# A hybrid decoder layer on one core: 2x2 block products for the convolution's inputs, one row of weight buffers, attention outputs kept in DRAM

## The chip, the core and the metric

The kernel runs on one core of a Trainium2 chip. The core has a matrix engine (TensorE, PE in the profile; its weight loads are shown as PEld), a vector engine (VectorE, DVE), a scalar engine (ScalarE, ACT), a general engine (GpSimd, POOL) and a queue engine (SyncE, SP). Each runs its own instruction queue in order, and they meet at semaphores. PE reads SBUF and accumulates into PSUM banks of 128 x 512 floats; DVE and ACT read and write both; DMA queues, fed here by SP and POOL, move data between DRAM and SBUF. The metric is the device time of one execution in microseconds (us), lower being better.

## What is computed

One decoder layer over 512 tokens with 16 learned meta tokens in front of them (528 positions), model width 2048, all in float32:

```python
n = _rmsnorm(h, g_mix[l])
p = n @ w_in[l]
q, k, v, gb, gc, u = jnp.split(p, ...)
o_attn = _stick_breaking_attention(q, k, v).reshape(b, L, ATTN_WIDTH)
o_conv = gb * _causal_dwconv(gc * u, conv_w[l])
o = jnp.concatenate([_rmsnorm(o_attn, g_attn_out[l]),
                     _rmsnorm(o_conv, g_conv_out[l])], axis=-1)
h = h + o @ w_out[l]
n2 = _rmsnorm(h, g_ffn[l])
h = h + (jax.nn.silu(n2 @ w_gate[l]) * (n2 @ w_up[l])) @ w_down[l]
return h[:, N_META:]
```

Each of q, k, v, b (`gb`), c (`gc`) and u is 1024 wide: 8 heads or channel blocks of 128. The convolution has three taps, so position t needs c*u at t-2, t-1 and t. The FFN is 5632 wide.

## The kernel before

**Layout and products.** Everything is held transposed: channels on the 128 partitions, tokens along the free axis. A float32 operand is split into a high part that PE takes in one pass (`float32r`) and the rest (a cast on ACT, a subtraction on DVE: `split`, L194). A product of weights W and activations a is the sum of W_hi a_hi, W_hi a_lo and W_lo a_hi: three matmuls for each 128 x 128 tile of weights and each stretch of up to 512 columns. The weights arrive as float32 by SP's queue and are split in the kernel as well.

**Stages**, in the order in which PE runs them:

- *Input.* x times `g_mix` is split into 16 pairs of tiles, `n_parts` (`nh`, `nl`, L226), one for each 128 of the 2048 model channels. The RMS factor `r` of each token and its square `r2` are applied to the products when they are taken out of PSUM.
- *Attention*, eight heads (`head`, L355): k, q and v by `product` (L190), which walks the 16 tiles of `n_parts`; then `attend` (L382), whose parts are threaded between the next head's matmuls by `after` and `tick`. Its output o (L491 to L496) is scaled and split into `oa_all`, which stays in SBUF until the output projection.
- *Convolution*, eight channel blocks (L532 to L560): c and u by `cu_product` (516 columns as 256 and 260: 16 tiles x 3 x 2 = 96 matmuls each), multiplied; three taps; b (512 columns, 48 matmuls); the product with b on POOL; the split into `oc_all`; the sum of squares `acc_c`. The parts of the last head's attention run under c, u and b of block 0. `scale_a` (L519) makes the attention group's RMS factor.
- *Output projection* (L562 and L839 on): for each of 16 output tiles one product over the attention half and one over the convolution half (48 matmuls of 512 columns in all), then the residual, and the activations of the FFN as *block products* want them.
- *FFN*: gate and up, then down, by `pair_product` (L756). It takes a 2 x 2 block matrix of weights times a 2 x 2 block matrix of activations (two halves of the contraction, two halves of the 512 tokens) in seven products of blocks instead of eight. For that, sums and differences of weight blocks (`add_quads`, `add_last`: four additions for each pair) are made on DVE, and sums and differences of activation blocks are kept beside the blocks themselves (`acts`, seven of them).

**Weights.** Until the first output tile, weights go through `stream`: tiles `raw` of eight 128 x 128 blocks (two of them), split in pieces of four blocks, four pieces ahead (`prepare`, L137; `next_w`, L152). From then on they go through two long tiles, `sw_in` (six places of eight blocks) and `sw_split` (three places for pairs of high and low parts), eight blocks at a time and two pieces ahead (`split_quad`, L651; `prepare_pair`, L677).

**Order.** The instructions are laid into each engine's queue by a scheduler that goes by the program's order, with preparation of weights at high priority. Space in SBUF is a stack of pools from either end: a pool opened where another was released waits, tile by tile, for what lay there (`reuse_waits="tile"`).

Of the kernel before, what the change touches and what calls it, by code (L numbers as in the profile page):

```python
# [15 lines left out]
P = 128  # L16
# [17 lines left out]
def hybrid_layer(ctx: ExitStack, tc: tile.TileContext, xT, w_in, w_out, w_gu, w_down, vecs, out):  # L34
# [67 lines left out]
    stream = []  # L102

    OUT_TILES = [k + 8 * half for k in range(8) for half in (1, 0)]

    WIDE_AT, PARTS_AT = 16, 48

    def plan_w(src, n, at=PARTS_AT):  # L110
        stream.append((src, n, at))

    FIRST = ((0, 2), (2, 4), (4, 8), (8, 12), (12, 16))
    for a, b in FIRST:
        for c in (8, 0):
            plan_w(w_in[c, a // 8][:, (a % 8) * P : (a % 8 + b - a) * P], b - a, PARTS_AT if c else WIDE_AT)
    for j in range(HEADS):
        for c in (8 + j, j, 16 + j)[0 if j else 2 :]:
            for b in range(2):
                plan_w(w_in[c, b], 8, WIDE_AT if c == j else PARTS_AT)  # L120
    for j in range(HEADS):
        for c in (32 + j, 40 + j, 24 + j):
            for b in range(2):
                plan_w(w_in[c, b], 8, WIDE_AT if c == 24 + j else PARTS_AT)
    for b in range(2):
        plan_w(w_out[OUT_TILES[0], b], 8)
    raws, ready, taken = [], [], [0]
    SUB, AHEAD = 4, 4
    subs = [(i, a, min(a + SUB, n)) for i, (_, n, _) in enumerate(stream) for a in range(0, n, SUB)]

    def load_raw(pool=wpool, cols=8 * P, **kw):
        i = len(raws)
        src, n, _ = stream[i]
        raws.append(pool.tile([P, cols], F32, name=f"raw{i}", **kw))
        tc.keep_in_program_order(nc.sync.dma_start(raws[i][:, : n * P], src))

    def prepare():  # L137
        i, a, b = subs[len(ready)]
        with tc.high_priority():
            if i == len(raws):  # L140
                load_raw(tag="raw", bufs=2)
            raw, c = raws[i][:, a * P : b * P], (b - a) * P
            at = stream[i][2]
            hi, lo = (
                wpool.tile([P, SUB * P + 64], F32R, tag=t, bufs=AHEAD + 1, name=f"{t}{i}_{a}")[:, at : at + c]
                for t in ("whi", "wlo")
            )
            sc.copy(hi, raw)  # L148
            ve.tensor_tensor(lo, raw, hi.bitcast(F32), ALU.subtract)  # L149
        ready.append((hi, lo, b - a))  # L150

    def next_w():  # L152
        i = taken[0]
        taken[0] += 1
        while len(ready) < min(len(subs), i + 1 + AHEAD):
            prepare()
        hi, lo, n = ready[i]
        return [(hi[:, k * P : (k + 1) * P], lo[:, k * P : (k + 1) * P]) for k in range(n)]
# [14 lines left out]
    def product_steps(parts, acts, n):  # L173

        k, last = 0, n - 1
        while k <= last:

            ws = next_w()
# [38 lines left out]

    accp = open_pool("accp")
    oapool = open_pool("oapool")
    rpool = open_pool("rpool", side="right")  # L220
    xpool = open_pool("xpool", KT, side="right")
    raw_first = open_pool("raw_first", side="right")
# [3 lines left out]
    n_parts = [[npool.tile([P, L + 48], F32R, name=f"{t}{k}") for t in ("nh", "nl")] for k in range(KT)]  # L226
    npool.tile([P, 8], F32, name="pad_n")
# [60 lines left out]

    for a, b in FIRST:
        for i in range(2):  # L290
            load_raw(raw_first, (b - a) * P)
            if a == i == 0:
                load_x(0)
        for k in range(max(a, 1), b):
            load_x(k)
    for a, b in FIRST:
        for k in range(a, b):
            split_x(k)
        for step in steps:
            next(step)  # L300
# [7 lines left out]
    raw_first.release()  # L308
# [11 lines left out]
    def o_slots(pool, name):  # L320

        t = pool.tile([P, 2 * HEADS * SEQ], F32R, name=name)
        return t.rearrange("p (h a t) -> p h a t", h=HEADS, a=2)

    oa_all = o_slots(oapool, "oa")
    oa = []

# [54 lines left out]
    def attend(h, kn, kh, kl, qn, qh, ql, vt):  # L382
# [98 lines left out]
        def mix(ws):  # L481
# [14 lines left out]
            oa.append((oh, ol))  # L496
# [22 lines left out]
    def scale_a():  # L519
        sh, sl = (tmp.tile([P, SEQ], F32R, tag=t, bufs=2, name=f"{t}_a") for t in ("e", "e2"))  # L520
        token_scale(acc_a, acc_a, 1024, "a", (sh, sl, t512(SEQ, "v", 2)[:, :SEQ], None, None))


    C0, CN = 12, L - 12
    oc = []

    def cu_product(name):
        ps = pp.tile([P, 2, 512], F32, tag="pp", name=name).rearrange("p a b -> p (a b)")
        product([(ps[:, T2:512], C0, C0 + T2), (ps[:, 512 : T2 + CN], C0 + T2, L)], n_hl)
        return ps[:, T2 : T2 + CN]  # L530

    for j in range(HEADS):  # L532
        pc = cu_product(f"pc{j}")
        cu = t512(CN, "e", 2)[:, :CN]
# [34 lines left out]
    wpool.release()  # L569
    npool.release()  # L570

# [560 lines left out]
```

## Time and profile before

| what | value |
|---|---|
| median of 3 runs | 2058.72 us (2058.11 to 2059.23) |
| span of the profiled execution | 2056.9 us |
| attention, first matmul of k to first of c of block 0 | 5.6 to 339.5 us |
| c and u of block 0 to the last b | 339.5 to 616.0 us |
| output projection | 616.0 to 790.6 us |
| FFN, gate and up | 790.6 to 1632.8 us |
| FFN, down | 1632.8 to 2053.1 us |

The profile is of one execution. Its span runs from the first to the last instruction; about 1.8 us of a run's time lie outside it. For each engine it gives the time in which it was busy. Matmuls are pipelined and their ends are modelled, so PE's busy time says that PE had work, not how fast it went; the pace is seen from the number of matmuls in a stretch. A row of instructions reads: line, engine, operation, output<-inputs, shapes, count | busy us, mean ns of one | idle time of the engine just before them, and what ended it. A row of DMA issues reads: destination<-source, queue, count, KB each, median us from issue to landing.

### The profile page before, as it was taken

What the parts mean: (1) busy time and instruction counts of PE and PEld (TensorE: products, weight loads), DVE (VectorE), ACT (ScalarE), POOL (GpSimd) and SP (SyncE); (2) the same over time, 40 slices, a digit from 0 to 9 for tenths busy, and PEclk for the clock granted to TensorE, in tenths of its full rate; (3) what the DMA queues carried; (4) which work ended last, traced back from release to release, by engine and by line L of the source; (5) the groups of instructions that cost most, each with busy time, mean ns of one, the idle gap of its engine ahead of it and who ended that gap; (6) DMA issues with size and microseconds to landing.
All of it is one profiled execution on the core that took longest, in us unless ns stands there. A gap on an engine that the chain in (4) does not pass through costs nothing.

```text
span 2056.9 us, 39370 instructions
## 1 busy us (share of the span) xinstructions
PE 2046.7 (100%) x16086; PEld 1976.0 (96%) x16086; DVE 1623.2 (79%) x2146; ACT 1016.0 (49%) x1529; POOL 351.5 (17%) x484
## 2 busy tenths in 40 slices
PE   9999999999999999999999999999999999999999
PEld 9899999999998888999999999999999999999999
DVE  7877767533336668999898898888888988888888
ACT  7666666322224344555555555555555544444443
POOL 0111111010103442111011011011011243131211
PEclk9999999999999999999999999999999999999999
DMA  5122222222235556556555465465455899798864
GB/s 198 63 83 72 80 75 76 94 93 93 95 103 168 169 173 201 160 148 190 155 162 166 145 176 158 148 175 154 144 175 164 257 338 348 186 300 208 218 149 94
DMA packets 141669, 326.74 MB, mean 159 GB/s; under 512 B 12256, under 2 KB 60128, under 8 KB 141488
## 3 DMA queue, kind: packets, MB, share of 16 engines
q1 hardware_dynamic: 67456, 212.50, 31.8%
q0 software_dynamic: 74032, 111.73, 21.1%
q8 instruction: 126, 2.06, 0.4%
q14 instruction: 55, 0.45, 0.1%
HBM read 258.91 MB, written 65.27 MB: 158 GB/s over the span
## 4 chain that ended last, share of the span: by engine, by line
PE 96%; DVE 2%; ACT 1%; issue 1%; DMA 0%; POOL 0%; SPq 0%; DVEq 0%; ACTq 0%; POOLq 0%
PE x L752 11%; PE x L754 11%; PE x L753 11%; PE z L752 6%; PE z L753 6%; PE z L754 6%; PE y L752 3%; PE y L753 3%; PE y L754 3%; PE po L732 3%; PE po L733 3%; PE po L731 3%; PE pv L182 2%; PE pv L184 2%; PE pv L183 2%; PE pu L184 1%
## 5 line engine op out<-in xcount | busy, mean ns | idle before, releaser
L654 ACT CAST sw_split<-sw_in 128x1024 fp32r<-128x1024 f32 (+1 forms) x534 | 526.4, 987 | 535.3 <-PE z L753 161.5
L655 DVE TENSOR_TENSOR sw_split<-sw_in,sw_split 128x1024 fp32r<-128x1024 f32 (+1 forms) x534 | 611.9, 1146 | 98.0 <-ACT sw_split L654 94.6
L752 PE MATMUL x<-f,sw_split 128*128 128x256 f32 x1408 | 387.6, 275 | 1.8 <-DVE u L787 1.5
L753 PE MATMUL x<-f,sw_split 128*128 128x256 f32 x1408 | 387.3, 275 | 0.2 <-DVE f L196 0.2
L754 PE MATMUL x<-f,sw_split 128*128 128x256 f32 x1408 | 387.2, 275 | 0.0
L752 PEld LDWEIGHTS x<-f,sw_split 128*128 128x128 f32 x1408 | 264.3, 188 | 2.3 <-DVE u L787 1.9
L753 PEld LDWEIGHTS x<-f,sw_split 128*128 128x128 f32 x1408 | 264.3, 188 | 0.4 <-DVE f L196 0.4
L754 PEld LDWEIGHTS x<-f,sw_split 128*128 128x128 f32 x1408 | 264.3, 188 | 0.0
L149 DVE TENSOR_TENSOR wlo<-raw,whi 128x512 fp32r<-128x512 f32 (+1 forms) x198 | 139.1, 706 | 127.4 <-ACT whi L148 126.9
L951 POOL DMA_DIRECT2D fd<-s x147 | 103.6, 911 | 709.7 <-DVE s L196 708.8
L148 ACT CAST whi<-raw 128x512 fp32r<-128x512 f32 (+1 forms) x198 | 121.1, 614 | 180.8 <-PE pu L183 64.1
L753 PE MATMUL z<-f,sw_split 128*128 128x256 f32 x704 | 193.6, 275 | 0.0
L752 PE MATMUL z<-f,sw_split 128*128 128x256 f32 x704 | 193.6, 275 | 0.0
L754 PE MATMUL z<-f,sw_split 128*128 128x256 f32 x704 | 193.6, 275 | 0.0
L661 DVE TENSOR_TENSOR sw_in<-sw_in 128x1024 f32<-128x1024 f32 (+1 forms) x144 | 163.4, 1134 | 5.5 <-DMA sw_in<-w_down 0.8
L754 PE MATMUL x<-ring,sw_split 128*128 128x256 f32 x608 | 167.3, 275 | 0.4 <-DVE sw_split L655 0.4
L753 PE MATMUL x<-ring,sw_split 128*128 128x256 f32 x608 | 167.2, 275 | 0.0
L752 PE MATMUL x<-ring,sw_split 128*128 128x256 f32 x608 | 167.2, 275 | 0.0
L753 PEld LDWEIGHTS z<-f,sw_split 128*128 128x128 f32 x704 | 132.2, 188 | 0.0
L752 PEld LDWEIGHTS z<-f,sw_split 128*128 128x128 f32 x704 | 132.2, 188 | 0.0
L754 PEld LDWEIGHTS z<-f,sw_split 128*128 128x128 f32 x704 | 132.2, 188 | 0.0
L754 PEld LDWEIGHTS x<-ring,sw_split 128*128 128x128 f32 x608 | 114.1, 188 | 0.6 <-DVE sw_split L655 0.6
(346 smaller groups left out, 5586.9 us busy)
## 6 DMA issues: line engine op xcount, KB each, us to landing
sw_in<-w_gu SPq DMA_DIRECT2D x176, 512.0 KB, 3.7
raw<-w_in SPq DMA_DIRECT2D x92, 512.0 KB, 3.3
fd<-s POOLq DMA_DIRECT2D x147, 256.0 KB, 5.2
sw_in<-w_down SPq DMA_DIRECT2D x96, 384.0 KB, 4.3
ring<-fd POOLq DMA_DIRECT2D x42, 768.0 KB, 17.2
sw_in<-w_out SPq DMA_DIRECT2D x30, 512.0 KB, 4.0
out_T<-d POOLq DMA_DIRECT2D x54, 256.0 KB, 4.8
sw_in<-w_down SPq DMA_DIRECT2D x16, 512.0 KB, 7.8
```

The costliest lines, as they stand in the source:

```text
L148: sc.copy(hi, raw)
L149: ve.tensor_tensor(lo, raw, hi.bitcast(F32), ALU.subtract)
L184: pe.matmul(ps, wl, ah[:, a:b], start=False, stop=k + i == last)
L654: sc.copy(hi, src)
L655: ve.tensor_tensor(lo, src, hi.bitcast(F32), ALU.subtract)
L661: return ve.tensor_tensor(sums[name], a, b, ALU.add)
L731: pe.matmul(ps, hi[:, kk], ah, start=k == 0, stop=False)
L732: pe.matmul(ps, hi[:, kk], al, start=False, stop=False)
L752: pe.matmul(p, hi[:, kk], act[:, 0, k], start=start and j == k == 0, stop=False, skip_group_check=skip)
L753: pe.matmul(p, hi[:, kk], act[:, 1, k], start=False, stop=False, skip_group_check=skip)
L754: pe.matmul(p, lo[:, kk], act[:, 0, k], start=False, stop=k == n - 1, skip_group_check=skip)
L951: gp.dma_start(fd[c][s][:, :, k], t[:, :, i])
```

## The change

1. *One row of weight buffers.* `hpool`, `sw_in` and `sw_split` are opened first and serve the whole program; `stream`, `wpool` and the tiles `raw` go. All weights are one list of `pieces`: the ten small ones of the start, "wide" ones of eight blocks, and seven for each pair. `n_parts` starts four elements into its tiles.
2. *Block products for c and u of blocks 1 to 7, and for b of blocks 2 to 7.* A pair of c and u (`conv_pair`) or of two b (`gate_pair`) takes seven block products of eight tiles: 168 matmuls, of 258 columns for c and u (each token half with the two positions in front of it) and 256 for b. c, u and b of block 0 and b of block 1 stay as they were. Of the seven activation blocks, three are mixtures that have to be made (`mix_x`): x is loaded again from DRAM, scaled by `g_mix`, and its quarters (two halves of the channels, two of the tokens) are added and subtracted and split into `mixed`. A fourth, `late`, overwrites a quarter of `n_parts` after the b product of block 1, the last that reads it.
3. *Attention outputs through DRAM.* Each head's output is split into a tile `st_o` and stored to DRAM; after the last pair, all eight are loaded into `oapool`, in the space that `mixed` had. The convolution's outputs are kept in float32 and split at the end.
4. *Around it.* The product with b and its sum of squares move from POOL to DVE (`gated`). `scale_a` comes after the second pair. The output projection starts with the attention halves of two tiles, then their convolution halves, and uses the PSUM banks of the pairs.

```diff
-    wpool = open_pool("wpool", side="right")
+    hpool = open_pool("hpool", side="right")
+    sw = open_pool("sw", side="right")
...
+    pairs = []
+    for j in range(1, HEADS):
+        pairs.append((8, [w_in[c + j, b] for b in range(2) for c in (32, 40)]))
+        if j >= CB and j % 2:
+            pairs.append((8, [w_in[c, b] for b in range(2) for c in (23 + j, 24 + j)]))
...
-    n_parts = [[npool.tile([P, L + 48], F32R, name=f"{t}{k}") for t in ("nh", "nl")] for k in range(KT)]
+    n_parts = [[npool.tile([P, L + 48], F32R, name=f"{t}{k}")[:, 4:] for t in ("nh", "nl")] for k in range(KT)]
...
-            oh, ol = oa_all[:, h, 0], oa_all[:, h, 1]
-            sc.activation(oh, o, AF.Copy, scale=g)
-            ve.scalar_tensor_tensor(ol, o, g, oh.bitcast(F32), ALU.mult, ALU.subtract)
+            st = stpool.tile([P, 2, SEQ], F32R, tag="st_o", bufs=2, name=f"st_o{h}")
+            sc.activation(st[:, 0], o, AF.Copy, scale=g)
+            ve.scalar_tensor_tensor(st[:, 1], o, g, st[:, 0].bitcast(F32), ALU.mult, ALU.subtract)
...
+            gp.dma_start(oa_dram[h], st)
...
-    for j in range(HEADS):
-        pc = cu_product(f"pc{j}")
...
+    def gated(p, j, y, gb, s):
+
+        ve.tensor_tensor(p, y, gb, ALU.mult)
+        square_sum(acc_c, p, j == 0, s, ve)
+        sc.activation(p, p, AF.Copy, scale=g_cnv[:, j : j + 1])
...
+    gb0 = t512(L, "v", 2)[:, :SEQ]
+    ve.tensor_tensor(gb0, pb[:, 0, :], r[:, META:], ALU.mult)
...
+    gated(ocf[0], 0, y0, gb0, t512(L, "r", 3)[:, :SEQ])
     tmp.release()
     const.release()
...
+    mixp = open_pool("mixp")
+    mixed = [mixp.tile([P, 8, 2, N], F32R, name=f"mixed{i}") for i in (1, 2, 3)]
+    ctmp = open_pool("ctmp", side="right")
...
+    def conv_acts(a=0, n=N):
+        return [
+            raw_block(0, 0, a, n),
+            *(mixed_block(t, a, n) for t in mixed),
+            last_block(a, n),
+            raw_block(1, 0, a, n),
+            raw_block(1, 1, a, n),
         ]
...
+    def mix_x(k):
+
+        x = []
+        for i in range(2):
+            if k % 2:
+                x.append(ctmp.tile([P, 3 * N], F32, tag="sides", name=f"x{k}_{i}") if i else ctmp.tile([P, CN], F32, tag="b0", name=f"x{k}_{i}"))
+                x[i] = x[i][:, :CN]
             else:
+                x.append(ctmp.tile([P, CN], F32, tag="cu", bufs=2, name=f"x{k}_{i}"))
+            gp.dma_start(x[i], xT[k + 8 * i][:, C0:])
+            sc.activation(x[i], x[i], AF.Copy, scale=g_mix[:, k + 8 * i : k + 8 * i + 1])
+        (a0, a1), (b0, b1) = ([t[:, i * T2 : i * T2 + N] for i in range(2)] for t in x)
+        d, e = (oc_slot(1 + m, F32, f"mix{k}_{m}")[:, :N] for m in (k % 2, 2))
+        ve.tensor_tensor(d, b1, a1, ALU.subtract)
+        split(mixed[0][:, k, 0], mixed[0][:, k, 1], d)
+        ve.scalar_tensor_tensor(e, d, -1.0, a0, ALU.mult, ALU.subtract)
+        split(mixed[1][:, k, 0], mixed[1][:, k, 1], e)
+        ve.scalar_tensor_tensor(d, e, -1.0, b0, ALU.mult, ALU.subtract)
+        split(mixed[2][:, k, 0], mixed[2][:, k, 1], d)
+        ve.tensor_tensor(late[:, k], a0, a1, ALU.subtract)
+
+    for k in range(8):
+        mix_x(k)
+    gb1 = oc_slot(7, F32, "gb1")
+    pb = pp.tile([P, 2, 512], F32, tag="pp", name="pb1")
+    product([(pb[:, 0, :], META, L)], n_hl)
...
+    for k in range(8):
+        split(*(n_parts[k][part][:, C0 + N : C0 + 2 * N] for part in range(2)), late[:, k])
...
+    def conv_pair(j):
+        u = ctmp.tile([P, CN], F32, tag="cu", bufs=2, name=f"cu{j}")
+        y, last = pair_product(conv_acts(), N, [u[:, t * T2 : t * T2 + N] for t in range(2)], [sides_c[:, t] for t in range(3)])
+        ve.tensor_tensor(u, u, r2[:, C0:], ALU.mult)
...
+    def gate_pair(j):
...
+    for j in range(1, HEADS):
+        conv_pair(j)
+        if j == 1:
+            gated(ocf[1], 1, ocf[1], gb1, gb1)
+        elif j == 2:
+            scale_a()
+        elif j % 2:
+            gate_pair(j)
+    mixp.release()
+    oapool = open_pool("oapool")
+    oa_all = [oapool.tile([P, 4, 2, SEQ], F32R, name=f"oa{i}") for i in range(2)]
+    for h in range(HEADS):
+        gp.dma_start(oa_all[h // 4][:, h % 4], oa_dram[h])
...
+    for part in range(2):
+        for i in range(2):
+            wide_product(ps_out[i][part], (oa, oc)[part])
```

A pair's blocks run in the order of `conv_acts`: a raw block, the three of `mixed`, the late one, two raw ones.

More of the change, by code (lines that the diff above doesn't have):

```diff
@@ L121, in hybrid_layer @@
[L121 to L135, printed above, removed]
+    acc_h = hpool.tile([P, SEQ], F32, name="acc_h")
@@ new lines, in hybrid_layer @@
+    for f in range(FT):
+        pairs.append(gate_up(f))
+    k0 = CHUNKS[0]
+    for j in range(KT // 4):
+        pairs.append(two_down(j, k0))
+    for n in CHUNKS[1:]:
+        for j in range(KT // 2):
+            pairs.append((n, [w_down[2 * j + m, k][:, k0 * P : (k0 + n) * P] for k in range(2) for m in range(2)]))
+        k0 += n
+    QUADS = ("11", "12", "22", "21")
+    SIX = CONV + FT + KT // 4
+    pieces = [("first", a, b) for a, b in FIRST for _ in range(2)]
+    n_first = len(pieces)
@@ L137, in prepare @@
+    FIRST_ORDER = (5, 0, 1, 2, 3, 4, 6)
     def prepare():
-        i, a, b = subs[len(ready)]
+        kind, i, s = pieces[len(split_w)]
         with tc.high_priority():
[L140 to L149, printed above, removed]
@@ L318, in hybrid_layer @@
     acc_a = accp.tile([P, SEQ], F32, name="acc_a")
[L320 to L326, printed above, removed]
+    stpool = open_pool("stpool")
+    oa_dram = [dram.tile([P, 2, SEQ], F32R, name=f"oa_dram{h}") for h in range(HEADS)]
     def qk_norm(read, dst, parts_of, name):
```

489 lines of the change are left out of this document (253 added, 236 removed).

## Prediction

> **What bounds the kernel now.** I read the page first: the busy shares and the chain that ended last.
>
> ```profile
> span 2056.9 us, 39370 instructions
> PE 2046.7 (100%) x16086; PEld 1976.0 (96%) x16086; DVE 1623.2 (79%) x2146; ACT 1016.0 (49%) x1529; POOL 351.5 (17%) x484
> ...
> PE 96%; DVE 2%; ACT 1%; issue 1%; DMA 0%; POOL 0%; SPq 0%; DVEq 0%; ACTq 0%; POOLq 0%
> ```
>
> The chain is PE from end to end, so time can only come from fewer or shorter matmuls, and every hole torn into PE's stream costs its full length. Next the waits of PE, to see how large holes are today.
>
> ```profile
> PE va L386 <- DVE tmp L379: 1.6, 1, 1.6
> PE x L752 <- DVE u L787: 1.5, 2, 1.3
> ...
> PE x L754 <- DVE sw_split L655: 0.4, 1, 0.4
> ```
>
> Columns: what waited, for what, us in total, times, the longest. The first two are the longest of all, the third is the only one for a split of weights: there are no holes to fill. A busy PE is not a pace, so I then took the table of stretches, cut so that one form of matmul fills a stretch. The columns after the length are busy us and instructions of PE, PEld, DVE, ACT and POOL, then clock, DMA share and GB/s.
>
> ```profile
> 324.94:331.48 6.54, 6.54 (x56) 6.54 (x54) 5.64 (x10) 5.30 (x10) 0.62 (x2) 1.00 0.24 80
> 413.93:436.72 22.79, 22.79 (x193) 22.79 (x192) 8.22 (x11) 6.10 (x10) 2.92 (x2) 1.00 0.29 93
> 436.72:447.61 10.89, 10.89 (x50) 9.01 (x49) 4.87 (x7) 3.21 (x5) 0.00 (x0) 1.00 0.30 98
> 616.01:790.60 174.59, 174.59 (x772) 144.54 (x771) 118.89 (x164) 70.43 (x119) 76.13 (x79) 1.00 0.52 167
> 900.00:1600.00 700.00, 700.00 (x6179) 700.00 (x6178) 627.41 (x701) 365.78 (x476) 90.62 (x129) 1.00 0.54 161
> ```
>
> In order: v of one head (264 columns, 54 matmuls: 121 ns each); c and u of one channel block (192 matmuls, half of 256 columns and half of 260: 118.7 ns each); its b (48 of 512 columns: 227 ns each); the output projection; the FFN, which already uses block products (256 columns: 113.3 ns each, or 0.443 ns a column). The FFN row also shows that seven-for-eight works here at 90% of VectorE with PE never short.
>
> **The change part by part.**
>
> *Fewer matmuls.* For j = 1 to 7, c and u cost 192 matmuls a pair now and 7 blocks x 8 tiles x 3 = 168 afterwards, of 258 columns. 258 is the mean of 256 and 260, so I take the 118.7 ns of that row: 19.94 us, a saving of 2.85, times 7 is **19.9 us**. Ends: at the FFN's 0.443 ns a column a matmul takes 114.3 ns and the seven save 25.1; at 122 ns (the v row and a little) they save 16.1. Three pairs of b cost 2 x 10.89 = 21.78 us each now and 168 matmuls of 256 columns afterwards; the moving blocks start at mixed offsets, so I put them between the FFN's 113.3 and the conv row's 118.7, at 116: 19.49 us, saving 2.29 x 3 = **6.9 us** (8.2 to 5.5). Together 26.8 us, between 33.3 and 21.6. The matmul records should go from 16086 to 16086 - 7 x 24 + 3 x 72 = 16134. Block 0 and the b of blocks 0 and 1 stay as wide products.
>
> *The mixed operands of x.* This is work that wasn't there: for each of 8 k, two DMAs of x by POOL, two ACT scalings of 514 columns, three splits (ACT cast, DVE subtraction) and four more DVE operations, all of 258 columns. Nearest rows:
>
> ```profile
> L655 DVE TENSOR_TENSOR sw_split<-sw_in,sw_split 128x1024 fp32r<-128x1024 f32 x366 | 451.5, 1234 | 70.4 <-ACT sw_split L654 68.9
> L661 DVE TENSOR_TENSOR sw_in<-sw_in 128x1024 f32<-128x1024 f32 x96 | 117.4, 1223 | 3.8 <-DMA sw_in<-w_down 0.8 <-DMA sw_in<-w_gu 0.7
> L196 DVE TENSOR_TENSOR s<-odd,s 128x1280 fp32r<-128x1280 f32 x22 | 32.6, 1484 | 0.2 <-ACT s L195 0.2
> L783 DVE SCALAR_TENSOR_TENSOR u<-z,sides 128x256 f32<-128x256 f32 x44 | 18.5, 420 | 8.9 <-PE z L754 8.9
> L196 DVE TENSOR_TENSOR s<-even,s 128x512 fp32r<-128x512 f32 x22 | 15.1, 684 | 0.0
> L196 DVE TENSOR_TENSOR w<-src,w 128x256 fp32r<-128x256 f32 x15 | 6.2, 411 | 0.0
> L547 DVE TENSOR_TENSOR tmp<-pb,r 128x512 f32<-128x512 f32 x8 | 5.5, 691 | 10.9 <-PE pb L184 10.9
> ```
>
> ```profile
> L885 ACT ACTIVATE src<-w,vec 128x512 f32<-128x512 f32 x16 | 11.6, 724 | 54.4 <-POOL w L884 30.6 <-DVE w L884 23.7
> L195 ACT CAST w<-src 128x256 fp32r<-128x256 f32 x15 | 6.0, 402 | 0.0
> L841 POOL DMA_DIRECT2D w<-xT x16 | 9.6, 599 | 19.7 <-ACT sw_split L654 13.8 <-DMA out_T<-w 3.6 <-ACT w L195 2.3
> ```
>
> ```profile
> w<-xT POOLq DMA_DIRECT2D x16, 256.0 KB, 3.5
> xt<-xT SPq DMA_DIRECT2D x16, 264.0 KB, 5.4
> ...
> f<-fx POOLq DMA_DIRECT2D x2, 1024.0 KB, 13.1
> ```
>
> Per k that is 7 x 0.42 = 2.94 us of DVE and 2 x 0.72 + 3 x 0.40 = 2.65 us of ACT; for 8 k, 23.5 and 21.2 us. Call T the end of block 0's b product. The x tiles are placed over the old temporaries, the last of which (`gb0`) falls free after one eviction and one product, T + 1.4; from there two issues of 0.60, a landing of 3.5 and two scalings bring DVE's first operation to T + 7.5. The first pair of tiles may find its space free about 3 us earlier, so I take T + 5. Weight preparation goes first on DVE: in this stretch four splits of 1.23 and three sums of 1.22, 8.6 us. So the first split of k = 7 is there at T + 5 + 23.5 + 8.6 - 1.7 (four operations that come after it) = T + 35.4. The cover is the b product of block 1 (10.9 us) and the first block of the first pair (2.8); the second block is the first on a mixed operand and reaches its k = 7 after another 2.5, at T + 16.2. PE would wait 19 us. Durations of neighbouring DVE operations overlap somewhat, so I take **17 us**. Ends: by the slope between the 512 and 1280 rows (1.04 ns an element, 0.27 us for 258) DVE's 56 operations are 15 us and a start at T + 2 leaves 8; at the other end the x tiles turn over only once for two k, a round being 2 x 0.60 + 5.4 (the slower landing) + 1.45 + some 3.3 of chain = 11.3 us, four rounds 45, which leaves 28. What is late next is absorbed: the other mixed blocks of k = 7 follow within 2 us, and the eight late splits (0.4 us each) have two blocks of PE time.
>
> *Attention outputs through DRAM.* Same ACT and DVE operations; one more POOL issue a head beside a POOL at 17%, and PE does not wait for it: the store's reader comes some 250 us later. The way back is eight loads of 512 KB, which may start when the last pair has left the first mixed tile, two blocks in (5.6 us), and the last is wanted after five more blocks and 4.8 us of the first output product, at about 24. Two loads of 1024 KB landed in 13.1 us, 160 GB/s: 4.2 MB would take 26 us, land at 32 and stop PE for 8; alone on the queues they would be faster than that by the half, and then nothing waits. I take **1 us** (0 to 8).
>
> *One row of weight buffers.* Splits of 8 tiles replace pairs of 4; the order and depth in tiles are alike, and the same DVE columns are subtracted. What hides a split is the work on the pieces split ahead, two of them, or 2 x 24 matmuls of 0.12 us; if that cover failed, PE would wait for the split, of which today's longest wait is 0.4 us. The activations start four elements later in their tiles, which may move the pace of the 1536 attention matmuls of 264 columns between 0.443 ns a column (117 ns) and a few ns above today's 121; no row prices it. I take 0 (6 us gained to 5 lost).
>
> *VectorE in the pairs.* A conv pair needs 7 x 1.23 + 4 x 1.22 = 13.5 us for weights and about 4.3 for its outputs (five operations of 0.42, one of 0.69, two of 0.75 as below), 17.8 of 19.9; a b pair about 19 of 19.5 by durations, which overlap, against the FFN's 90%. I put 0, and if the 0.19 us that each split waits for its cast (70.4 over 366) were added, three b pairs would lose 0.9 each.
>
> ```profile
> L541 DVE SCALAR_TENSOR_TENSOR tmp<-tmp,vec,tmp 128x512 f32<-128x512 f32 x16 | 12.0, 751 | 1.7 <-ACT tmp L539 1.4
> ```
>
> **Sum** against the execution's own 2056.9: - 26.8 + 17 + 1 = 2048.1. The median of the runs lies 1.8 above the span, so **2050 us**, 0.4% faster.
>
> A rule that speaks against the change stands in the Trainium skill, "TensorE: Matmul & The Clock Gate", Part 1: after an idle window of about 3.4 us PE drops to half clock, and needs about as long of sustained work to come back. The granted clock is 1.00 in every stretch here, but no wait above 1.6 us occurs, so no row of this trace tests it. By it the hole would cost another 1.7 us, half of 3.4, an estimate from that page.
>
> **The rivals.**
>
> *Slow restart.* A PE that has idled may run slow at first, as it does at the start of the program:
>
> ```profile
> L82 PE MATMUL warm<-ones 128*128 128x128 f32 x20 | 4.6, 429 | 1.1 <-DVE one L78 1.1
> L406 PE MATMUL z<-qn,kn 128*128 128x144 f32 x16 | 3.3, 285 | 0.0
> ```
>
> The first 20 matmuls took 4.6 us and 429 ns each, against 285 ns for a longer FP32 one in mid-program. If half of the 4.6 us is loss, the same after the hole costs 2.3 us: 2052. The rule named above is the same mechanism.
>
> *The hole is much smaller*, because engines fill it earlier than I think. For: DVE is busy 8.2 of 22.8 us in today's conv stretch and could start mixing under b. Against: the tiles that x needs are not free before. With 4 us instead of 17: 2037.
>
> *A late return of the attention outputs*, 160 GB/s as in the row above, 7 us more: 2057.
>
> *Slower than before*: the x tiles' turnover. If landing takes 5.4 instead of 3.5 us and only two k are in flight, the four rounds of 11.3 us end the mixing at T + 45 and PE waits 29: 2056.9 - 26.8 + 29 + 1 + 1.8 = 2062, and up to 2068 if rounds are 12.8. It decides from a hole of 26 us, rounds of about 10.5. For it: SP's loads of the same rows took 5.4 when they came in a row, as these will; against: POOL's own took 3.5.
>
> **How the numbers follow.** Forecast (2043 to 2056) 0.42; slow restart 0.12; small hole 0.15; late return 0.13; slower 0.18. The likeliest is 2050 with 2043 to 2056 of its own. With the pace at the FFN's and a small hole it goes to 2036, with the slow rounds to 2064: that range leaves out about 2 in 10. A change of 0.2% (4.1 us) is what a measurement tells from none. Faster by more: the small hole, most of the forecast and of the restart, 0.67; within: 0.17; slower: most of the last case, 0.16.
>
> **What would show it.** Matmul count 16134; a stretch of 168 matmuls per pair of 19.9 us (c, u) and 19.5 us (b); one hole in PE, right after the b product of block 1, with DVE's split of a mixed tile as releaser and about 17 us in pieces of some 3 us, one for each k; no wait above 2 us at the output projection; output projection, FFN and down stretches of the same length as before. I am wrong if the hole is under 8 or over 28 us, if PE waits for splits inside the pairs, or if the pace of 258 columns is far from 118.7 ns.

## The result, and the profile after

The changed kernel takes 2066.83 us (median of 5 runs, 2065.66 to 2070.4) against 2058.74 of the kernel before on the same chip: ratio 1.0041, interval 1.0028 to 1.0054. It is 0.4% slower; the forecast was 2050 us, faster than before, with 2064 at the top of its range.

The head of the page of the changed kernel, and its chain of waits:

```profile
span 2065.1 us, 39541 instructions
PE 2034.2 (99%) x16134; PEld 1968.8 (95%) x16134; DVE 1744.4 (84%) x2243; ACT 1071.1 (52%) x1551; POOL 347.0 (17%) x501
...
PE 91%; DVE 3%; DMA 3%; ACT 1%; issue 1%; SPq 0%; POOL 0%; DVEq 0%; ACTq 0%; POOLq 0%
```

PE has the 16134 matmuls that were foretold and is busy 12.5 us less than before, yet the span is 8.2 us longer: PE is idle for 21 us more, and DMA, absent from the chain before, now has 3% of it. The five stages, in the table of stretches (start:end, length, then busy us of PE, PEld, DVE, ACT, POOL, clock, DMA share, GB/s), cut at the first matmul of the convolution, of the output projection, of gate and up, and of down; first the kernel before, then the changed one:

```profile
0.00:339.45 339.45, 336.13 (x2266) 312.94 (x2266) 258.63 (x477) 218.98 (x401) 44.80 (x108) 1.00 0.28 93
339.45:616.01 276.56, 276.56 (x1963) 260.82 (x1962) 119.09 (x177) 87.21 (x146) 25.73 (x29) 1.00 0.28 94
616.01:790.58 174.57, 174.57 (x771) 144.53 (x770) 118.89 (x164) 70.41 (x119) 76.13 (x79) 1.00 0.52 167
790.58:1632.79 842.21, 839.78 (x7396) 838.63 (x7395) 760.63 (x860) 442.16 (x580) 115.08 (x163) 1.00 0.56 167
1632.79:2056.90 424.11, 419.63 (x3698) 419.07 (x3696) 366.00 (x469) 197.28 (x285) 89.73 (x106) 1.00 0.85 234
```

```profile
0.00:343.71 343.71, 338.30 (x2265) 312.85 (x2266) 258.72 (x431) 214.85 (x354) 46.71 (x115) 1.00 0.32 106
343.71:621.75 278.04, 260.81 (x2012) 253.37 (x2010) 228.97 (x313) 142.36 (x212) 18.92 (x40) 0.96 0.37 120
621.75:796.74 174.99, 174.90 (x772) 144.37 (x771) 130.56 (x175) 73.16 (x122) 75.09 (x77) 1.00 0.54 167
796.74:1640.58 843.84, 840.31 (x7395) 838.99 (x7394) 760.26 (x858) 443.35 (x580) 116.31 (x165) 1.00 0.56 167
1640.58:2065.10 424.52, 419.91 (x3698) 419.27 (x3696) 365.93 (x469) 197.39 (x285) 89.94 (x106) 1.00 0.85 234
```

By stage the change costs 4.3 us up to the convolution, 1.5 in it, 0.4 in the output projection, 1.6 in gate and up and 0.4 in down: 8.2 in all. The convolution is where something should have been gained: PE is busy 15.8 us less there and idle 17.2, and the mean clock is 0.96. The longest waits of PE and the stretches of the first pair, of a later c and u pair and of a b pair show it:

```profile
PE z L766 <- ACT mixed L315: 10.2, 3, 5.1
PE z L766 <- DVE gb L732: 5.6, 1, 5.6
PE pv L302 <- ACT tmp L397: 2.3, 1, 2.3
PE x L766 <- ACT sides_c L786: 1.5, 1, 1.5
```

```profile
396.01:440.53 44.52, 27.29 (x169) 24.70 (x168) 35.66 (x74) 25.18 (x50) 5.99 (x12) 0.73 0.39 118
461.09:481.40 20.31, 20.31 (x169) 20.31 (x168) 19.33 (x25) 9.84 (x13) 0.00 (x0) 1.00 0.32 104
481.40:501.10 19.70, 19.70 (x171) 19.70 (x170) 17.09 (x21) 10.05 (x13) 0.00 (x0) 1.00 0.32 105
```

A pair without a wait takes 20.31 us; the first takes 44.52. The **hole is 24.2 us**, and the granted clock is 0.73 in the mean over that pair. The savings, by the last two rows and those of the kernel before, are 7 x (22.79 - 20.31) + 3 x (21.78 - 19.70) = 23.6 us: the one eats the other, and nearly all of the loss that is left lies outside the convolution.

In time, the loads of x on POOL and three operations of DVE (start, length, engine, line; in brackets what ended the idle time before it). The b product of block 0 ends at 384.8, that of block 1 at 395.8:

```profile
384.81 0.56 POOL L715 DMA_DIRECT2D x<-xT  x1
387.87 1.60 POOL L715 DMA_DIRECT2D x<-xT  x3 [2.50 <-DVE p L649]
395.54 0.54 POOL L715 DMA_DIRECT2D x<-xT  x1 [6.08 <-ACT mixed L315]
```

```profile
392.43 0.42 DVE L725 TENSOR_TENSOR late<-x 128x258 f32<-128x258 f32 x1
...
403.86 0.69 DVE L732 TENSOR_TENSOR gb<-pb,r 128x512 f32<-128x512 f32 x1
...
422.62 0.42 DVE L723 SCALAR_TENSOR_TENSOR mix<-mix,x 128x258 f32<-128x258 f32 x1
```

Three of the first four loads wait for `gated` of block 0 (its product `p`, L649) to leave the old temporaries; the fifth waits 6.1 us more for a tile of x to be free. DVE mixes from 392.4 to 423.0, and the eviction of block 1's b stands 8 us in its queue, although its product is long done.

At the start, ACT in the changed kernel, and the first head's v product:

```profile
29.62 2.94 ACT L202 CAST sw_split<-sw_in 128x1024 fp32r<-128x1024 f32 x3 [3.35 <-PE pk L304]
32.47 0.60 ACT L396 ACTIVATE tmp<-pk 128x528 f32<-128x528 f32 x1
```

```profile
33.71:47.00 13.29, 13.29 (x96) 13.29 (x97) 9.23 (x14) 8.18 (x14) 0.00 (x0) 0.87 0.45 147
```

Three wide casts stand ahead of the read of k, whose PSUM bank v needs. v starts at 33.71 instead of 30.39, and runs 13.29 instead of 11.68 us, at a clock of 0.87.

### The profile page after: what moved, and what is told of

It reads as the page before. It is cut to its first block, busy times and chain, and to the rows that moved or that the text cites. A ratio compares the mean times of both kernels' runs of the same rounds, so it can differ in the third digit from the quotient of the medians.

```text
span 2065.1 us, 39541 instructions
## 1 busy us (share of the span) xinstructions
PE 2034.2 (99%) x16134; PEld 1968.8 (95%) x16134; DVE 1744.4 (84%) x2243; ACT 1071.1 (52%) x1551; POOL 347.0 (17%) x501
## 4 chain that ended last, share of the span: by engine, by line
PE 91%; DVE 3%; DMA 3%; ACT 1%; issue 1%; SPq 0%; POOL 0%; DVEq 0%; ACTq 0%; POOLq 0%
PE x L766 13%; PE x L768 13%; PE x L767 13%; PE z L767 6%; PE z L766 6%; PE z L768 6%; PE y L767 3%; PE y L766 3%; PE y L768 3%; PE pv L302 2%; PE pv L303 2%; PE pv L304 2%; PE pq L303 1%; PE pq L304 1%; PE pq L302 1%; PE pk L302 1%
## 5 line engine op out<-in xcount | busy, mean ns | idle before, releaser
L202 ACT CAST sw_split<-sw_in 128x1024 fp32r<-128x1024 f32 (+2 forms) x668 | 661.9, 992 | 708.8 <-PE z L767 190.8
L203 DVE TENSOR_TENSOR sw_split<-sw_in,sw_split 128x1024 fp32r<-128x1024 f32 (+2 forms) x668 | 771.6, 1156 | 165.2 <-ACT sw_split L202 156.8
L209 DVE TENSOR_TENSOR sw_in<-sw_in 128x1024 f32<-128x1024 f32 (+1 forms) x164 | 187.9, 1146 | 10.4 <-DMA sw_in<-w_gu 3.2
L768 PEld LDWEIGHTS x<-ring,sw_split 128*128 128x128 f32 x608 | 114.1, 188 | 0.7 <-DVE sw_split L203 0.7
L766 PEld LDWEIGHTS x<-ring,sw_split 128*128 128x128 f32 x608 | 114.1, 188 | 0.0
L767 PEld LDWEIGHTS x<-ring,sw_split 128*128 128x128 f32 x608 | 114.1, 188 | 0.0
```

Of the source, the lines that this page charges most:

```text
L202: sc.copy(hi, src)
L203: ve.tensor_tensor(lo, src, hi.bitcast(F32), ALU.subtract)
L209: return ve.tensor_tensor(sums[name], a, b, ALU.add)
L766: pe.matmul(p, hi[:, kk], ah, start=start and j == k == 0, stop=False, skip_group_check=skip)
L767: pe.matmul(p, hi[:, kk], al, start=False, stop=False, skip_group_check=skip)
L768: pe.matmul(p, lo[:, kk], ah, start=False, stop=k == n - 1, skip_group_check=skip)
```

## The experiments

Each was timed against the kernel before on the same chip, whose medians were 2058.5 to 2059.1 in all of them. Stretches of the first pair are measured as above, each in the one execution that was profiled. The mixing's code is the same in the changed kernel and in two of the runs below (early reads, scratch moved), and their first pairs take 44.5, 45.3 and 45.8 us: differences of about a microsecond between two traces show nothing.

**No mixing.** The loop over `mix_x` and the late splits are gone, `conv_acts` takes plain blocks:

```diff
-    for k in range(8):
-        mix_x(k)
...
-            *(mixed_block(t, a, n) for t in mixed),
-            last_block(a, n),
+            *(raw_block(0, 0, a, n) for _ in mixed),
+            raw_block(0, 1, a, n),
```

> Leaves out the mixed operands of x: no loads, scalings, differences and splits for them, and the block products of the pairs read the plain halves of x in their place (same number and length of matmuls). Theory (the whole loss in the convolution is PE waiting for the mixing, 24.2 us in the first pair): 2066.8 - 24.2 = 2042.6 us, first pair 20.3 us long like the others, no clock below 1.00 there, and the rest of the excess, 4.9 us at the start and some 2 us near the output projection and the first gate and up products, stays. Rival (the hole only moves to another wait, for example for weights, or the pairs are slower than 20.3 us for another reason): 2050 us or more.

2042.0 us, ratio 0.992 (0.9907 to 0.9934). The first pair:

```profile
395.26:416.00 20.74, 20.74 (x170) 20.74 (x169) 15.71 (x17) 7.89 (x10) 0.00 (x0) 1.00 0.46 157
```

No hole and full clock: 24.8 us of the total hang on the mixing, as the theory had it. This kernel doesn't compute the layer, since its pairs multiply plain blocks where mixed ones belong.

**What sets the length of the mixing?** Four runs. First the eviction of block 1's b at high priority:

```diff
+    with tc.high_priority():
-    ve.tensor_tensor(gb1, pb[:, 0, :], r[:, META:], ALU.mult)
+        ve.tensor_tensor(gb1, pb[:, 0, :], r[:, META:], ALU.mult)
```

> The eviction of block 1's b product goes ahead of the mixing on VectorE; nothing else is changed. Theory (VectorE's sum of work for the mixing sets the end; the wait of 5.6 us for this eviction is only the first piece of the hole): the piece of 5.6 us goes, the later pieces grow by nearly as much, total within 1 us of the changed kernel, 2066 to 2067. Rival (the eviction that sits behind the mixing holds PE up by itself, since its PSUM bank is reused): 5.6 us less, 2061.

2066.0 us (1.0037, 1.0024 to 1.0050): without the longest single wait 0.8 us are gained by the medians, within the noise. It was not a cause of its own. Its 5.6 us are gone from the waits of PE, but those for `mixed` grow from 10.2 to 13.8, and the first pair still takes 44.74 (columns as above):

```profile
PE z L767 <- ACT mixed L315: 13.8, 6, 3.4
```

Then x is loaded for two k only, and the later mixtures are made of the wrong x:

```diff
+    xs = {}
...
     def mix_x(k):
...
-        x = []
-        for i in range(2):
+        x = xs.setdefault(k % 2, [])
+        for i in range(0 if k > 1 else 2):
...
+        for i in range(2):
```

> x is loaded for the first two k only, and the later six reuse those tiles (scaled again); scalings, differences and splits stay, so the mixed operands of k = 2 to 7 are wrong. Theory (VectorE's and ScalarE's work sets the length of the mixing, transfers are mostly hidden): VectorE's idle time for x in the stretch is 2 to 3 us in all, so 2064 to 2067. Rival of the prediction (the turnover of the x tiles, landing included, sets the rounds): 10 us or more off, 2057 or less.

2060.3 us (1.0009, 1.0000 to 1.0017): 6.5 off, between the two; the first pair takes 38.3 us. The late splits behind the last mixed one:

```diff
-        split(mixed[2][:, k, 0], mixed[2][:, k, 1], d)
         ve.tensor_tensor(late[:, k], a0, a1, ALU.subtract)
+        sc.copy(mixed[2][:, k, 0], d)
+        return ve.tensor_tensor(mixed[2][:, k, 1], d, mixed[2][:, k, 0].bitcast(F32), ALU.subtract)
...
-        mix_x(k)
+        last_mix = mix_x(k)
...
+      with tc.issue_after(last_mix.ins):
         split(*(n_parts[k][part][:, C0 + N : C0 + 2 * N] for part in range(2)), late[:, k])
```

> The eight late splits (wanted five blocks later) are issued after the last split of a mixed tile instead of in between; same work. Theory (VectorE is busy nearly all of the mixing, so what stands ahead of the last mixed split sets it): 7 or 8 of them at 0.34 us go behind, 2.5 us less, 2064 us. Rival (they only filled time in which VectorE waited for x or a cast): 2066 to 2067, with VectorE's idle time in the stretch grown by what was moved.

2067.0 us (1.0043, 1.0030 to 1.0056): nothing gained. The stretches from DVE's first operation on x (a `late` or a `mix`) to its last, of the changed kernel, with x loaded once, and with the late splits behind:

```profile
392.43:423.04 30.61, 14.88 (x65) 11.64 (x63) 27.66 (x69) 22.03 (x49) 6.45 (x12) 0.68 0.42 121
```

```profile
390.79:414.60 23.81, 14.76 (x65) 11.51 (x63) 23.81 (x62) 21.07 (x48) 0.00 (x0) 0.69 0.08 24
```

```profile
390.99:421.65 30.66, 15.00 (x65) 11.64 (x63) 25.36 (x61) 22.12 (x49) 6.47 (x12) 0.67 0.42 121
```

The DVE column decides. Without reloads DVE is busy every one of 23.8 us: that is the floor that its work sets. In the changed kernel the mixing takes 30.6, with 27.7 busy, and with the eight late splits taken out it takes 30.7, with 5.3 idle: they had only filled time in which DVE waited. So what lies above the floor, 6.8 us, is set by the **turnover of the x tiles**: two k in flight, each wanting its last reader done, an issue of 0.54 us on POOL, a landing of 3.1 and a scaling in ACT's queue; in the mean over the four rounds, 7.7 us each. My theory for these two runs, that DVE's and ACT's work alone sets the length, was wrong by that.

Last, the late differences and the subtractions of their splits on POOL:

```diff
-        ve.tensor_tensor(late[:, k], a0, a1, ALU.subtract)
+        gp.tensor_tensor(late[:, k], a0, a1, ALU.subtract)
...
-        split(*(n_parts[k][part][:, C0 + N : C0 + 2 * N] for part in range(2)), late[:, k])
+        split(*(n_parts[k][part][:, C0 + N : C0 + 2 * N] for part in range(2)), late[:, k], gp)
```

> The eight differences for the last block and the subtractions of their splits, 16 of the 56 VectorE operations of the mixing, go to GpSimd. Theory (VectorE's sum of operations sets the pace): 16 x 0.34 = 5.4 us less, 2061.5. Rival (the chain through x's landing, scaling and the casts sets it, with VectorE busy only because it has the late splits to fill in; the loads of x are issued on GpSimd too and now wait behind these operations): no gain or a loss, 2066 to 2070.

2069.1 us (1.0051, 1.0037 to 1.0065), the rival: the first pair grows from 44.5 to 47.2 us. POOL, which issues the loads that the turnover waits for, is now busy 18.9 of the 31 us of mixing and not 6.5; that this is the cause is likely, but no run separates it.

**The clock in the hole.**

```diff
+                for _ in range(16 if warm_up is not None and k else 0):
+                    tc.keep_in_program_order(pe.matmul(warm_up, hi[:, kk], raw_block(0, 0)(0, k), start=True, stop=True, skip_group_check=True))
...
-        block_product(z, acts[1], True)
+        block_product(z, acts[1], True, y if i == 0 else None)
```

> Block 1's eviction first, as in the run for it, and 16 matmuls of 258 columns (1.9 us) into a bank not yet in use between every two tiles of the first block on a mixed operand, where PE waits some 3 us a tile: work that nothing reads, so that PE is never idle for 2 us. Theory (the holes cost a second time, because the clock drops to 0.5 in them and stays there after the last one): granted clock 1.00 through the stretch, the block after the hole takes 2.9 us and its wait for the copy of 1.5 instead of 5.2, so 1 to 2.5 us less than the 2066.0 of the run without them: 2063.5 to 2065. Rival (the drop only falls into time in which PE waits anyway): the same time or up to 1 us more, since a tile can come while the extra matmuls run.

2064.5 us (1.0029, 1.0018 to 1.0040). Block 1's eviction is first here too, so it is compared with that run (2066.0); the two intervals overlap. First pair without and with the extra matmuls:

```profile
394.64:439.38 44.74, 28.42 (x169) 24.89 (x168) 35.15 (x75) 25.33 (x50) 6.00 (x12) 0.73 0.39 118
```

```profile
394.15:436.90 42.75, 37.52 (x281) 35.86 (x280) 35.10 (x74) 25.32 (x50) 5.97 (x12) 0.96 0.42 124
```

112 matmuls more on PE, and the stretch is 2.0 us shorter, with the mean clock at 0.96 instead of 0.73. The gain lies behind the hole: the last five blocks of the pair take 14.6 us with the extra matmuls, as much as in a pair without a wait, and 16.8 without them, since the clock is still at 0.50 when they start. So the hole is paid a second time through the clock, by 2.3 us here; in the trace of the changed kernel, where the clock came back sooner, the five blocks take 15.9, a loss of 1.3.

**A block more of cover, free of charge.**

```diff
-            n, swapped = pairs[i][0], i == CONV
+            n, swapped = pairs[i][0], i in (0, CONV)
...
-        first = i == CONV
+        first = i in (0, CONV)
```

> In the first pair of the convolution the block on the second half of x, which needs no mixed operand, goes ahead of the others, as the first pair of the gate and up products does; same work. Theory (a block more of cover comes off the hole one for one): 2.9 us less, 2064 us. Rival (PE then takes weights sooner, and the splits of these go ahead of the mixing on VectorE, so that the end of the mixing moves back by about two splits and a sum): 0 to 1 us less.

2066.2 us (1.0037, 1.0024 to 1.0050): the rival. Measured as above, the mixing now takes 33.0 us (391.43 to 424.38) instead of 30.6, so most of the 2.9 us of cover is given back, and the first pair still takes 44.8.

**Three wide b products over the mixing**, alone and with the reads of the first head early. In both the output projection's scratch overwrites a sum of weights of the first gate and up pair, which is made before the scratch was last used, so that pair's output is wrong; gate and up take 839.9 us and not 843.8 there, which fits a sum that doesn't wait for the scratch.

```diff
-    CB = 2
+    CB = 4
...
+    for j, i in ((1, 7), (2, 5), (3, 4)):
+        gbs[j] = oc_slot(i, F32, f"gb{j}")
+        pb = pp.tile([P, 2, 512], F32, tag="pp", name=f"pb{j}")
+        product([(pb[:, 0, :], META, L)], n_hl)
+        with tc.high_priority():
+            ve.tensor_tensor(gbs[j], pb[:, 0, :], r[:, META:], ALU.mult)
```

> The b of blocks 2 and 3 stay two wide products and run straight after the b of block 1, so that three wide products of 10.9 us lie over the mixing of x instead of one; the evictions of the three go first on VectorE. Price: 2 x 10.9 - 19.7 (a b pair) = 2.1 us. Theory (the mixing is work of about 37 us behind the end of block 0's b, whatever PE does meanwhile): the cover grows from 16.2 to 38.0 us, the hole goes from 24.2 to 0 to 2 us, 2066.8 - 24.2 + 2.1 + 1 = 2045.7 us. Rival (wide products feed VectorE as much weight work as they give cover, so that the mixing stretches along): half of the hole stays, 2055 or more.

> The three wide b products over the mixing, and the reads of the first k and q ahead of two of the wide casts at the start. Theory (the two losses add): the time of the version with the b products alone less 1.6 us, the gain measured for the reads alone: 2044 us, below the 2058.6 of the kernel before. Rival (part of the gain of the reads was the clock of that run and not the order): no difference between the two.

2047.9 us (0.9945, 0.9933 to 0.9958) and 2045.4 (0.9936, 0.9924 to 0.9949). The first pair takes 26.74 and 27.35 us: of 21.8 us of cover, 17 to 18 come off the hole. The rest is given back by the mixing, which takes 35.0 us instead of 30.6, with DVE, which now has the weights and evictions of three wide products, busy for 34.0 of them.

**The start.**

```diff
+    with tc.high_priority(1 << 20):
-    read_k0, read_q0 = read_qk(halves(pk0, H), g_k, L), read_qk(pq0[:, 0, :], gq_s, SEQ)
+        read_k0, read_q0 = read_qk(halves(pk0, H), g_k, L), read_qk(pq0[:, 0, :], gq_s, SEQ)
```

> The reads of the first head's k and q products come ahead of two of the three wide weight casts on ScalarE; work is the same. Theory (the one row of weight buffers lets wide casts run ahead at the start, they hold up the read of k, and with it the first v product by 2.5 us, after which the clock is at 0.5 for 3.4 us): the hole and the slow stretch go, 2 to 4 us, 2063 to 2065. Rival (the wide weights land late and PE would wait for their splits instead, 28.3 to 31.0 us): same time within 1 us, 2066 to 2067, with a wait for weights in place of the wait for the read.

2065.2 us (1.0036, 1.0023 to 1.0050), 1.6 less with intervals that overlap. In its trace v starts at 31.99 instead of 33.71 and runs 11.75 us at clock 1.00 instead of 13.29, and the convolution starts 2.4 us sooner, at 341.34. All the traces together are clearer: the convolution starts at 340.7 to 341.7 us in the five kernels with early reads (this one and four below), and at 341.9 to 343.7 in the changed kernel and the nine others without, so the order is worth 1.4 us in the mean and the changed kernel's own trace is the slowest start of all. Between the early reads and the 339.45 of the kernel before, 1.9 us remain. Some 0.5 of these are a slower pace: from the fourth head on a head takes 41.87 us, with early reads or without, and 41.76 before.

**The combination, and the start of gate and up.** Three wide b products, late splits behind, the block on the second half of x first, early reads; sums of quadrants placed so that they keep off the scratch:

```diff
-        sums[name] = w_place(sw_in, n, (4 if n == 8 else 6) + ((name == "t3") ^ i % 2))
+        sums[name] = w_place(sw_in, n, (4 if n == 8 else 6) + ((name == "t3") ^ (i - CONV) % 2))
```

> Together: three wide b products over the mixing, late splits behind it, the block on the second half of x first, the reads of the first k and q ahead of two wide casts; the sums of weight quadrants start their two places anew at the first gate and up pair, so that they keep off the scratch of the output projection. Theory (what was left of the hole, 6 to 7 us with the clock at 0.5 in it, is covered by 2.9 of a block and 2.5 of late splits): 2045.4 less 5 = 2040.5 us, first pair within 2 us of 20.3 and no drop of the clock there. Rival (VectorE stays full, so that weights and mixing just change places and PE waits for weights): 2044 to 2046.

2050.9 us (0.9962, 0.9948 to 0.9976), above both. The first pair takes 25.1 us, but gate and up take 846.9 instead of the changed kernel's 843.8. The longest wait of DVE at their start, in the combination and in the changed kernel:

```profile
DVE sw_in L209 <- DMA sw_in<-w_gu: 3.9, 1, 3.9
```

```profile
DVE sw_in L209 <- DMA sw_in<-w_gu: 2.6, 1, 2.6
```

A sum of the second pair waits on DVE for weights, and splits of activations that PE needs queue behind it. Those weights are loaded when the first pair's sum has read their place, and that sum waits for the scratch `t1`, `t2` of the output projection, which lies in the sixth weight place. Two runs move the scratch into a tile of its own stage, in the combination and in the changed kernel; a third does it for the three wide b products and early reads alone:

```diff
+        sq, t2 = (src[:, a : a + 2].rearrange("p a b -> p (a b)") for a in (4, 2 * half))
         def residual(eng):
+            t1 = sq
...
-            square_sum(acc_h, hj, i == 0, t1)
+            square_sum(acc_h, hj, i == 0, sq if half else wide_tmp("st", F32, 2))
```

> The combination of the run before (three wide b products over the mixing, late splits behind it, the block on the second half of x first, early reads at the start), but the output projection's scratch lies in a tile of its own stage instead of the sixth weight place, and the sums of quadrants are not started anew. Theory (in the combination, 7 us were lost at the start of gate and up against the version with the three b products, because a sum of quadrants waits for the scratch, the next pair's weights are loaded only after it, and a sum on VectorE that waits 3.9 us for these stands ahead of the splits that PE needs): 2050.9 less 5 to 7 = 2044 to 2046 us. Rival (the 7 us come from the other order of the first pair): 2050 to 2051.

> The changed kernel with the scratch of the output projection in a tile of its own stage, nothing else. Theory (VectorE's wait of 2.6 us for the second pair's weights at the start of gate and up comes from the sum that waits for the scratch, as above): the stretch from the first gate and up matmul to the last is 843.7 us and goes to 840, so 3 to 4 us less, 2063 us; the hole in the convolution stays at 24. Rival: the same time within 1 us.

> The three wide b products over the mixing, the early reads and the scratch of its own; the first pair and the late splits in the order of the changed kernel. Theory (covering the mixing is worth what the first pair shows, 44.5 - 27.3 = 17 us, less 2.1 for the two wide b products, plus 1.6 at the start and 3.7 at the start of gate and up): 2066.8 - 17.2 + 2.1 - 1.6 - 3.7 = 2046.4 us; the combination with the block on the second half of x first and the late splits behind is 2 us below it. Rival (that block and the late splits only move VectorE's work about): both within 0.5 us of each other.

The changed kernel with its scratch moved takes 2063.3 us (1.0025, 1.0017 to 1.0034), 3.5 less; DVE no longer waits for weights there, and gate and up take

```profile
796.20:1636.49 840.29, 839.15 (x7395) 838.46 (x7394) 759.78 (x858) 442.66 (x580) 116.11 (x165) 1.00 0.56 167
```

which is 3.5 us less than in the changed kernel and 1.9 less than in the kernel before: the theory holds. The combination with it takes **2045.3 us (0.9937, 0.9925 to 0.9950)**, the three wide products alone 2048.2 (0.9949, 0.9935 to 0.9963). Both beat the kernel before, the first by 13.2 us, and the changed kernel by 21.5. Their first pairs:

```profile
415.56:442.70 27.14, 22.17 (x169) 21.34 (x167) 25.76 (x43) 14.57 (x28) 0.63 (x2) 0.96 0.39 118
```

```profile
416.05:445.41 29.36, 23.90 (x170) 23.10 (x169) 23.54 (x39) 13.12 (x23) 0.54 (x1) 0.88 0.27 87
```

The combination has 2.2 us less of hole and the higher clock (0.96 against 0.88). Whether the block first and the splits behind, worth nothing by themselves, are worth something once the hole is short is not shown: the medians lie 2.9 us apart, but the intervals overlap, and in the earlier run with the three products and early reads, whose convolution has the order of the kernel with 29.36, the first pair took 27.35. Some 7 us of hole are left, now partly a wait for weights (2.3 us for a split, the longest).

## Why the prediction was wrong

**Which steps held.** The matmul count (16134); the hole's place, right after block 1's b, with splits of mixed tiles as its releasers; nothing waits at the output projection (0.1 us of idle PE in its 175 us); PE waits for no split inside the later pairs; the pace of gate and up is unchanged away from its start.

**The savings**, 26.8 forecast, came to 23.6. The step was the pace: 258 columns were put at 118.7 ns a matmul, the mean of the old pair; they take 20.31/168 = 120.9. 256 columns were put at 116 and take 19.70/168 = 117.3. 3.2 us, inside the given ends (33.3 to 21.6).

**The mixing**, 17 forecast, tore a hole of 24.2, inside the ends of 8 and 28. This is the term that was mis-sized most, and the step that failed is the pace of the mixing: after its start it was added up as DVE's work alone, with the turnover of the x tiles kept for a rival. The experiments show both: DVE's work makes 23.8 us, the turnover stretches it to 30.6. In the working, three things were too kind. (1) The start: T + 7.5 was worked out, and T + 5 taken because the first tiles might be free sooner; one of four loads was, DVE began at T + 7.6. (2) "Durations overlap somewhat, so I take 17": its own sum gave 19. Operations do follow each other at 0.34 us and not 0.42, and between its first operation on x and k = 7's first split DVE had two splits and two sums of weights, 4.9 us, and not 8.6; but the turnover used up what both gave, and k = 7's first split came at T + 37.4. That this lies so near to the T + 35.4 of the sum is luck: two sizes were too high by about as much as the turnover, left out of the sum, then added. Against PE's T + 16.2 it is a hole of 21. (3) The rest, 3 us, is what follows the last piece: the clock, 1.3 in this trace, and a wait of 1.5 for a copy (`sides_c`) that stands behind the mixing on ACT.

**The rivals.** The one that ended slower, the turnover, was the right mechanism at two thirds of its size: rounds of 7.7 us, not 11.3. It was said to decide only from a hole of 26; a hole of 24.2 was enough, because of the savings above and the start below. The slow restart was right as well, and not a rival but an addition. The Trainium skill, "TensorE: Matmul & The Clock Gate", Part 1, named it; by its rule 1.7 us were estimated, and 1.3 were measured in the changed kernel, 2.3 in the run with block 1's eviction first. Two things were made alternatives that happened together.

**What stood at nothing.** The row of weight buffers was costed by its splits in steady state only, "today's longest wait is 0.4". But wide splits run ahead wherever places are free, also at the start, where ACT's queue carries the reads that free PSUM. The start cost 4.3 us in this trace, of which the early reads bring back 2.4. At the start of gate and up 1.6 us came on; there a wait for weights stands behind a sum that needs the scratch's place. The kernel before has that scratch too, and why it costs more now is open. Neither was looked for, since the prediction named what hides a split on PE and not who else stands in ACT's and DVE's queues. The pace of the attention matmuls, put at 0, is a small loss: with `n_parts` starting four elements later, v at full clock takes 11.74 to 11.76 us in all the changed kernels' traces and 11.67 before. That the start of the tiles is the reason is not shown.

The sum of the errors: 3.2 (savings) + 7.2 (hole) - 0.6 (return, 0.4 for 1) + 4.3 + 1.6 + 1.3 (small waits in convolution and down) = 17.0 us, between 2048.1 and 2065.1.

**Open**: what is left of the 1.9 us of the start beyond the slower heads; a third k of x in flight wasn't tried, so the turnover is shown only by leaving the reloads out.

## What to carry to other kernels

Work put ahead of a stage costs its latency chain (free a tile, issue, land, scale, split) and not its sum on the busiest engine, so count rounds of buffers first, then look for independent work of the bounding engine to lay over them: here two products kept in the dearer form, 2.1 us more by their lengths, took 17 off the hole. A wait that ends last names one queue entry; moving the eviction alone gave 0.8 us here, within the noise, as the next entry was nearly as late. When a buffer is shared by the whole program, look at the places where stages meet, and at what else lies in it.

## What the runs showed of the hardware

The granted clock can drop after waits of 2 us, and no fixed length decides. Ahead of the first v product, PE waited 2.3 us in the changed kernel, 2.1 in the run with POOL's late splits and 2.0 without the mixing; each time the clock then stood at 0.50 for about 3.4 us, and v took 13.3 us. Waits of 1.4 to 1.6 us left it alone (11.7 us), and so did waits of 2.0 in the runs with extra matmuls and with the scratch moved. Elsewhere a wait of 1.8 us, at the start of gate and up in the run with block 1's eviction first, was followed by a drop, and waits of 2.3 us for the same split in the first pair were followed by one in the combination with its scratch moved and not in the combination before. The Trainium skill, "TensorE: Matmul & The Clock Gate", Part 1, speaks of an idle window of about 3.4 us that runs freely; here 1.8 to 2.3 us of waiting were sometimes enough.

At full clock, the same matmul of 258 columns took between 118.5 and 123.4 ns, by block and nearly the same for a block's place in the pair, and 256 columns took 117.3 ns in the mean of a b pair (113.3 to 121.3 by block) against 113.3 in the long stretch of gate and up. Without the mixing, where every block reads a plain half of x, 256 columns took 113.3 ns in the blocks of the b pairs and 258 took 123.3 in most of the c and u pairs. So the pace goes with what a block reads; why wasn't tried.
